# Every other load of expert weights is issued from ACT instead of SyncE

## The chip, the core and the metric

The kernel runs on one core of a Trainium2 chip. The core has a matrix engine (PE; its weight loads are shown apart as PEld), a vector engine (DVE), a scalar engine (ACT), GpSimd (POOL) and SyncE (SP), each with an instruction stream of its own that runs in order; they wait for one another through semaphores. DMAs bring data from HBM into the on-chip memory; the instruction that starts one stands in the stream of some engine, and in this kernel nearly all of them stand in SP's. The metric is the time of one execution in microseconds (us), as the median of several runs.

## The reference

Two residual layers over 256 tokens of width 1024. Each layer mixes tokens (a forgetting attention of 16 heads beside a gated recurrence of 8 heads), and then mixes channels. Layer 0 has a dense SwiGLU; layer 1, where the change lies, has eight SwiGLU experts of width 3584, of which each token uses its best two:

```
logits = (t @ w_router).astype(F32) + b_router.astype(F32)
top_val, top_idx = lax.top_k(logits, TOP_K)
top_w = jax.nn.softmax(top_val, axis=-1)
combine = jnp.sum(jax.nn.one_hot(top_idx, N_EXPERTS, dtype=F32) * top_w[..., None], axis=1)
for e in range(N_EXPERTS):
    out = out + combine[:, e:e + 1] * swiglu(t, w_gate[e], w_up[e], w_down[e]).astype(F32)
```

All weights are float32: one expert has three matrices of 1024 x 3584, some 44 MB, and all eight are read in full.

## The kernel before

Matrix products are made from float32 numbers split into a high and a low part, each in the format that PE multiplies at full rate. A piece of weights of 128 x 2048 numbers (1 MB) is loaded into a buffer `raw`; ACT casts a half of it (128 x 1024) to the high part `whi` (line 93), DVE subtracts that from `raw` to get the low part `wlo` (line 97), and PE multiplies with both (`mm3`, lines 113 to 115: high by high, high by low, low by high).

The experts are taken in an order set at run time, by how many tokens each has. Of the eight turns, those numbered 1, 4 and 7 (`FEW`) hold at most 64 tokens: there the high and the low part of the tokens share one block of 128 columns, and a weight needs two products instead of three (lines 1502, 1503, 1525, 1526). They are called the short turns here, the other five the long turns.

The experts' work is one list, `parts`, of 332 pieces, each of 1 MB of weights: for a block of 1024 hidden columns four parts of the gate matrix ("g"), four of the up matrix ("u"), and four of the down matrix of the block before ("d"). The function `run` writes the instructions out in a fixed order. In pass m it emits the products of part m, then the cast and the subtraction for the first half of part m + 2, then those for its second half; small operations (activation, transposes, gather, scatter) are hooked in between at three slots. `whi` and `wlo` have four buffers each, that is, two parts.

The buffers `raw` form a ring of 13 in the experts' stage. The load of part m + 13 overwrites the buffer of part m, so it waits for DVE's subtraction of the second half of part m, the last reader. The function `loads` emits, at the end of each pass, whatever loads have become possible; all of them stand in SP's stream (line 86). When the list comes to a new expert, SP reads that expert's number from memory into a register (line 1795), from which the addresses follow.

Of the kernel before, what the change touches and what calls it, by code (L numbers as in the profile page):

```python
# [10 lines left out]
F32 = mybir.dt.float32  # L11
# [6 lines left out]
P = 128  # L18
D = 1024
# [8 lines left out]
NE = 8  # L28
# [12 lines left out]
def hybrid_trunk_kernel(  # L41
# [6 lines left out]
    nc = tc.nc  # L48
# [16 lines left out]
    ring = [[wraw], 0, []]  # L65

    def raw_tile():
        pools = ring[0]
        j = ring[1] % sum(n for _, _, n, *_ in pools)
        if ring[1] and not j and ring[2]:  # L70
            pool, tag, bufs = ring[2].pop(0)
            return pool.tile([P, 2048], F32, tag=tag, bufs=bufs, name="raw")
        ring[1] += 1
        for pool, tag, n, *bufs in pools:
            if j < n:
                return pool.tile([P, 2048], F32, tag=tag, bufs=(bufs or [n])[0], name="raw")
            j -= n

    def load_raw(src, nk, n, step=None):
        raw = raw_tile()  # L80
        if nk * n == 2048:
            raw = raw.rearrange("p (k n) -> p k n", k=nk)
        else:
            raw = raw.rearrange("p (k n) -> p k n", k=max(4, nk))[:, :nk, :n]
        for k in range(0, nk, step or nk):
            nc.sync.dma_start(out=raw[:, k:k + (step or nk)], in_=src[:, k:k + (step or nk)])
        return raw

    def halves(raw, room=None):

        hi, lo = room or (wp.tile([P, 2, 512], F32R, tag=t, bufs=NSP, name=t) for t in ("whi", "wlo"))
        hi, lo = hi[:, :raw.shape[1], :raw.shape[2]], lo[:, :raw.shape[1], :raw.shape[2]]
        a.copy(hi, raw)  # L93
        return raw, hi, lo

    def lower(raw, hi, lo):
        v.tensor_sub(lo, raw, hi.bitcast(F32))  # L97

    def pairs_of(w):
        return [(w[1][:, j], w[2][:, j]) for j in range(w[1].shape[1])]  # L100
# [1114 lines left out]
    def moe(l, gate0):  # L1215
        with tc.tile_pool(name="moe", bufs=1, reuse_waits="tile") as mp:
# [130 lines left out]
            def an_expert(cl, w, **kw):  # L1347
                return dict(pos=cl[0], sel=cl[1], comb=cl[2], w=w, **kw)
# [84 lines left out]
            consts = {}  # L1433
# [247 lines left out]
            def run(exs):  # L1681
                parts, hooks = [], {}
# [5 lines left out]
                def hooked(key, slot):  # L1688
                    for f, args in hooks.pop((key, slot), ()):
                        f(*args)  # L1690
# [24 lines left out]
                for at, (ex, J) in enumerate(order):  # L1715
                    e, nq = ex["e"], ex["blocks"][J][1] // 256
# [45 lines left out]
                e, w_ = ex["e"], ex["blocks"][last][1]  # L1762
# [8 lines left out]
                key = (e, last, "d", 1, 0)  # L1771
# [9 lines left out]
                raws, ws = {}, {}  # L1781
                nring, once = sum(n for _, _, n, *_ in ring[0]), len(ring[2])
                known = [exs[0]]

                def loads(done):

                    while len(raws) < len(parts):
                        m = len(raws)
                        n = m + 3
                        prev = n - nring - (once if n < 2 * nring + once else 0)  # L1790
                        if n >= nring + once and prev - 3 > done:
                            break
                        e = parts[m]["key"][0]
                        if e == len(known):
                            r = nc.values_load(consts["idi"][0:1, e:e + 1], engines=(mybir.EngineType.SP,), min_val=0, max_val=NE - 1)
                            exs[e]["w"] = [w[0, bass.ds(r, 1)].rearrange("o d f -> (o d) f") for w in (moe_w_gate, moe_w_up, moe_w_down)]
                            known.append(exs[e])
                        src = parts[m]["src"]()
                        if src.shape[1] == 2:
                            raws[m] = load_raw(src, 2, D).rearrange("p k (h n) -> p (k h) n", h=2)  # L1800
                        else:
                            raws[m] = load_raw(src, 4, 512, 2 if m >= len(parts) - LASTS else 4)

                def half(m, k):
                    if m < len(parts):
                        w = halves(raws[m][:, k:k + 2])
                        lower(*w)
                        ws.setdefault(m, []).extend(pairs_of(w))

                loads(-1)  # L1810
                for m in range(2):
                    half(m, 0)
                    half(m, 2)
                    loads(m)
                    if m == 0:
                        silu(exs[0], 0, 0)
                        times_up(exs[0], 0, 0)
                for m, p in enumerate(parts):
                    p["products"](ws.pop(m))
                    hooked(p["key"], 0)  # L1820
                    half(m + 2, 0)
                    hooked(p["key"], 1)
                    half(m + 2, 2)
                    hooked(p["key"], 2)
                    loads(m + 2)
# [4 lines left out]
            exs = [an_expert([[t[:, i, 0:1] for i in range(NT)] for t in (pos, sel, comb)], [w[0, 0] for w in (moe_w_gate, moe_w_up, moe_w_down)],  # L1830
                             e=0, few=False, blocks=narrow)]
            for e in range(1, NE):
                exs.append(an_expert([[consts[k][:, i, e:e + 1] for i in range(NT)] for k in ("pos", "sel", "comb")], None, e=e, few=e in FEW, blocks=wide))
            with tc.manual_schedule():
                begin(exs[:1])
                run(exs)
# [72 lines left out]
LASTS = 2  # L1909
# [26 lines left out]
```

## Time and profile before

| | |
|---|---|
| median of 3 runs | 1940.73 us (1937.63 to 1941.56) |
| the profiled execution | 1939.08 us |
| its span, first to last instruction | 1937.4 us |
| PE busy | 1806.3 us, 93% |
| DVE busy | 1588.0 us, 82% |
| ACT busy | 1310.3 us, 68% |
| HBM read | 522.72 MB |

Busy time is time in which an engine runs instructions; issuing a DMA and waiting are not counted. A busy share over the whole span mixes stages with different limits, so the rows further down are taken from stretches of the experts' stage, which runs from about 936 to 1926 us. The program has the same instructions on PE, DVE and POOL before and after.

### The profile page before, as it was taken

To read this page: it belongs to the slowest core of one execution; us is meant where nothing else is said; L and a number is where in the kernel's file an instruction comes from. 1 tells how busy PE (TensorE), PEld (TensorE's weight loads), DVE (VectorE), ACT (ScalarE), POOL (GpSimd) and SP (SyncE) were. 2 spreads that over 40 slices of the span, in tenths; PEclk is the share of its full clock that TensorE was granted. 3 is DMA by queue.
4 is the path that set the end of the run, shared out by engine and by line. 5 is a ranking of instruction groups with operands and counts; after the bars stand their busy time and mean duration, and the time that the engine had idled before them with its cause. 6 is when DMAs were issued, how large, how long until landed. Compare 5 with 4: busy or idle time off the path is not lost. (4 is left out here: it accounts for less than half of the span.)

```text
span 1937.4 us, 25438 instructions
## 1 busy us (share of the span) xinstructions
PE 1806.3 (93%) x9038; PEld 1445.8 (75%) x9038; DVE 1588.0 (82%) x2061; ACT 1310.3 (68%) x1688; POOL 226.8 (12%) x214
## 2 busy tenths in 40 slices
PE   2999999999999999999999889999998899999887
PEld 2787787889978877788786557888865578878554
DVE  6877865878857877457888999989999999898997
ACT  2466568554445665685678778777787877777785
POOL 6701100000000012000211000310003200011000
PEclk9999999999999999999899999999999999999999
DMA  9534554788945425336989999989999899999991
GB/s 298 185 134 152 196 174 151 284 303 302 320 183 186 144 89 172 109 136 256 348 298 337 348 357 389 355 325 360 371 364 341 318 374 368 364 361 332 353 361 53
DMA packets 171399, 525.50 MB, mean 271 GB/s; under 512 B 11756, under 2 KB 23292, under 8 KB 157184
## 3 DMA queue, kind: packets, MB, share of 16 engines
q1 hardware_dynamic: 169880, 523.61, 75.1%
q8 instruction: 73, 1.20, 0.2%
q14 instruction: 62, 0.51, 0.1%
q10 hardware_dynamic: 1384, 0.18, 0.1%
HBM read 522.72 MB, written 1.05 MB: 270 GB/s over the span
## 5 line engine op out<-in xcount | busy, mean ns | idle before, releaser
L97 DVE TENSOR_TENSOR wlo<-raw,whi 128x1024 fp32r<-128x1024 f32 (+1 forms) x888 | 1071.2, 1237 | 142.2 <-ACT whi L93 132.5
L93 ACT CAST whi<-raw 128x1024 fp32r<-128x1024 f32 (+1 forms) x888 | 907.4, 1046 | 302.9 <-PE acc L115 160.4
L114 PE MATMUL acc<-wlo,g 128*128 128x512 f32 x544 | 213.8, 393 | 4.9 <-DVE wlo L97 4.9
L113 PE MATMUL acc<-whi,hTh 128*128 128x512 f32 x512 | 211.5, 415 | 4.4 <-ACT hTh L615 4.1
L113 PE MATMUL acc<-whi,g 128*128 128x512 f32 x544 | 215.2, 396 | 0.0
L114 PE MATMUL acc<-wlo,hTh 128*128 128x512 f32 x512 | 208.0, 407 | 6.3 <-DVE wlo L97 6.2
L115 PE MATMUL acc<-whi,g 128*128 128x512 f32 x544 | 213.1, 392 | 0.0
L115 PE MATMUL acc<-whi,hTl 128*128 128x512 f32 x512 | 208.8, 408 | 3.4 <-DVE hTl L617 3.4
L1503 PE MATMUL acc<-wlo,g 128*128 128x512 f32 x336 | 144.3, 430 | 32.8 <-DVE wlo L97 32.5
L1502 PE MATMUL acc<-whi,g 128*128 128x512 f32 x336 | 134.7, 401 | 1.2 <-ACT whi L93 1.2
L1503 PEld LDWEIGHTS acc<-wlo,g 128*128 128x128 f32 x336 | 63.0, 188 | 87.2 <-DVE wlo L97 77.9
L114 PEld LDWEIGHTS acc<-wlo,g 128*128 128x128 f32 x544 | 102.7, 189 | 29.3 <-DVE wlo L97 8.9
L115 PEld LDWEIGHTS acc<-whi,g 128*128 128x128 f32 x544 | 102.5, 188 | 21.5
L114 PEld LDWEIGHTS acc<-wlo,hTh 128*128 128x128 f32 x512 | 98.6, 193 | 26.8 <-DVE wlo L97 9.1
L113 PEld LDWEIGHTS acc<-whi,g 128*128 128x128 f32 x544 | 102.6, 189 | 20.8
L411 PE MATMUL acc<-hTh,whi 128*128 128x256 f32 x416 | 117.4, 282 | 0.0
L413 PE MATMUL acc<-hTh,wlo 128*128 128x256 f32 x416 | 116.7, 281 | 0.0
L412 PE MATMUL acc<-hTl,whi 128*128 128x256 f32 x416 | 116.6, 280 | 0.0
L115 PEld LDWEIGHTS acc<-whi,hTl 128*128 128x128 f32 x512 | 97.9, 191 | 24.7 <-DVE hTl L617 5.3
L113 PEld LDWEIGHTS acc<-whi,hTh 128*128 128x128 f32 x512 | 97.7, 191 | 23.7 <-ACT hTh L615 5.0
L114 PE MATMUL yb<-wlo,th 128*128 128x512 f32 x280 | 111.8, 399 | 2.2 <-DVE wlo L97 2.2
L302 POOL TENSOR_TENSOR rs<-rs,mhalf 128x8 f32<-128x8 f32 (+1 forms) x28 | 50.9, 1818 | 532.0 <-DVE rs L301 502.4
(421 smaller groups left out, 3203.6 us busy)
## 6 DMA issues: line engine op xcount, KB each, us to landing
raw<-in_moe_w_gate SPq DMA_DIRECT2D x112, 1024.0 KB, 7.3
raw<-in_moe_w_up SPq DMA_DIRECT2D x112, 1024.0 KB, 7.0
raw<-in_moe_w_down SPq DMA_DIRECT2D x110, 1024.0 KB, 6.9
raw<-in_w_in SPq DMA_DIRECT2D x66, 1024.0 KB, 5.1
raw<-in_w_ada SPq DMA_DIRECT2D x48, 1024.0 KB, 6.6
raw<-in_dense_w_gate SPq DMA_DIRECT2D x10, 1024.0 KB, 8.4
raw<-in_dense_w_up SPq DMA_DIRECT2D x10, 1024.0 KB, 7.5
raw<-in_dense_w_down SPq DMA_DIRECT2D x10, 1024.0 KB, 8.5
```

The lines of the kernel that those rows point to most:

```text
L93: a.copy(hi, raw)
L97: v.tensor_sub(lo, raw, hi.bitcast(F32))
L113: pe.matmul(out=o, lhsT=lh, rhs=rh, start=start, stop=False)
L114: pe.matmul(out=o, lhsT=lh, rhs=rl, start=False, stop=False)
L115: pe.matmul(out=o, lhsT=ll, rhs=rh, start=False, stop=stop)
L302: g.tensor_tensor(out=r, in0=r, in1=mhalf[:, :shape[1]], op=OP.pow)
L411: pe.matmul(out=o, lhsT=hi, rhs=hT.hh[:, k], start=(k == 0 and c % 2 == 0), stop=False)
L412: pe.matmul(out=o, lhsT=hi, rhs=hT.hl[:, k], start=False, stop=False)
L413: pe.matmul(out=o, lhsT=lo, rhs=hT.hh[:, k], start=False, stop=(k == KD - 1 and c % 2 == 1))
L1502: pe.matmul(out=o, lhsT=ex["g"][:, k], rhs=hi, start=(k == 0), stop=False)
L1503: pe.matmul(out=o, lhsT=ex["g"][:, k], rhs=lo, start=False, stop=(k == KD - 1))
```

## The change

`loads` is split into two queues. Each odd part from 13 on is loaded by an instruction in ACT's stream, every other part by one in SP's as before. The ring, the buffers and the sizes stay; the buffer of a part is now computed from its number, because the two queues no longer take them strictly in turn.

```
+                    raws[m] = raw.rearrange("p (k n) -> p k n", n=512)
+
+                turns_of = [m + 3 >= nring + once and m % 2 for m in range(len(parts))]
+
+                def loads(done, second=0):
+
+                    while at[second] < len(parts):
+                        m = at[second]
+                        if turns_of[m] == second:
+                            if needs(m) > done:
+                                break
+                            load(m, (nc.sync, nc.scalar)[second])
+                        at[second] += 1
...
                     p["products"](ws.pop(m))
                     hooked(p["key"], 0)
                     half(m + 2, 0)
+                    loads(m + 1, 1)
                     hooked(p["key"], 1)
                     half(m + 2, 2)
                     hooked(p["key"], 2)
                     loads(m + 2)
```

`needs(m)` is the number of the part that had the buffer last, so in the steady state m - 13. The new call stands between the two halves of a pass: in pass m, with m odd, ACT gets its cast for the first half of part m + 2, then the load of part m + 14, then the cast for the second half. That load waits for DVE's subtraction of the second half of part m + 1. ACT also reads each new expert's number into a register of its own (line 1797).

On ACT, in the first block of the short turn 4, the stream had six casts in a row between the activation of line 1556 and the copy of line 1564:

```order
L1556 ACTIVATE hid<-hid 64x1024
L93 CAST whi<-raw 128x1024 x6
L1564 COPY ug<-acc 64x512
L93 CAST whi<-raw 128x1024
L1564 COPY ug<-acc 64x512
```

and now has at the same place, with ISA the register arithmetic for the address:

```order
L1556 ACTIVATE hid<-hid 64x1024
L93 CAST whi<-raw 128x1024 x2
L1810 ISA
L1810 DMA raw<-in_moe_w_down 128x2048
L93 CAST whi<-raw 128x1024 x4
L1810 ISA
L1810 DMA raw<-in_moe_w_down 128x2048
L1564 COPY ug<-acc 64x512
L93 CAST whi<-raw 128x1024
L1564 COPY ug<-acc 64x512
```

Two loads have come in, four casts apart; the casts themselves have kept their order.

On SP, where the loads pass from one expert to the next (the fourth time), the stream had

```order
L86 DMA raw<-in_moe_w_down 128x2048
L1795 TENSOR_LOAD rank
L1795 ISA x2
L86 ISA
L86 DMA raw<-in_moe_w_gate 128x2x1024
L86 ISA
L86 DMA raw<-in_moe_w_gate 128x2x1024
L86 ISA
L86 DMA raw<-in_moe_w_gate 128x2x1024
```

and now has

```order
L1810 DMA raw<-in_moe_w_down 128x2048
L1797 TENSOR_LOAD rank
L1797 ISA x2
L1810 ISA
L1810 DMA raw<-in_moe_w_gate 128x2x1024
L1810 ISA
L1810 DMA raw<-in_moe_w_gate 128x2x1024
L1810 ISA
L1810 DMA raw<-in_moe_w_up 128x2x1024
```

The gate matrix now comes as two loads on SP, with two more on ACT, where it came as four on SP. In all 161 load instructions stand on ACT: 160 odd parts from 13 to 331, the last of them in two halves.

## Rows read from the trace of the kernel before

**Rows 1.** The page: busy time of each engine.
```profile
PE 1806.3 (93%) x9038; PEld 1445.8 (75%) x9038; DVE 1588.0 (82%) x2061; ACT 1310.3 (68%) x1688; POOL 226.8 (12%) x214
```
**Rows 2.** Stretches, long, short, whole stage: length, busy PE, PEld, DVE, ACT, POOL, clock, DMA.
```profile
1330.00:1420.00 90.00, 89.70 (x402) 73.70 (x401) 83.67 (x80) 70.45 (x76) 3.11 (x2) 1.00 0.98 359
1455.00:1547.00 92.00, 74.60 (x287) 50.38 (x285) 84.32 (x83) 72.66 (x92) 26.31 (x14) 0.94 0.92 331
936.50:1926.00 989.50, 920.34 (x3923) 700.95 (x3921) 906.99 (x888) 775.45 (x885) 101.20 (x63) 0.99 0.92 339
```
**Rows 3.** Waits of PE, 936 to 1926: total us, times, longest us.
```profile
PE acc L1503 <- DVE wlo L97: 32.5, 52, 1.2
PE yb L1526 <- DVE wlo L97: 21.1, 19, 1.9
...
PE acc L114 <- DVE wlo L97: 4.9, 7, 2.2
```
**Rows 4.** Waits of ACT, the two longest, and of DVE, 936 to 1926.
```profile
ACT whi L93 <- PE acc L115: 53.3, 139, 2.9
ACT whi L93 <- PE yb L115: 48.8, 109, 1.7
...
DVE wlo L97 <- ACT whi L93: 71.7, 121, 2.8
```
**Rows 5.** Waits of SP, the longest, 936 to 1926.
```profile
SPq L86 <- DVE wlo L97: 755.3, 314, 9.3
```
**Rows 6.** Line 86, 936 to 1926: ns min/median/max of an issue; last, us to landing.
```profile
L86 SPq DMA_DIRECT2D raw<-in_moe_w_down x112: 328/345/384, 949.5 to 1887.5; - x112
...
L86 SPq DMA_DIRECT2D raw<-in_moe_w_gate x103: 368/383/412, 936.2 to 1864.3; - x103
...
DMA to landing us min/median/max: 4.8/7.0/8.9
```
**Rows 7.** Timeline of ACT around 26: start us, us, engine, line, work.
```profile
26.26 0.43 ACTq L235 DMA_DIRECT2D og<-in_hg_o_gain  x1
26.38 1.04 ACT L93 CAST whi<-third 128x1024 fp32r<-128x1024 f32 x1
...
27.19 0.46 ACTq L237 DMA_DIRECT2D wr<-in_w_router  x1
27.69 1.04 ACT L93 CAST whi<-raw 128x1024 fp32r<-128x1024 f32 x1 [0.27 <-issue]
```
**Rows 8.** Timeline of DVE, SP and ACT around 1441, short turn 4.
```profile
1440.25 1.23 DVE L97 TENSOR_TENSOR wlo<-raw,whi 128x1024 fp32r<-128x1024 f32 x1 [0.93 <-ACT whi L93]
...
1441.50 0.35 SPq L86 DMA_DIRECT2D raw<-in_moe_w_down  x1
...
1441.07 1.04 ACT L93 CAST whi<-raw 128x1024 fp32r<-128x1024 f32 x1
...
1442.53 1.22 DVE L97 TENSOR_TENSOR wlo<-raw,whi 128x1024 fp32r<-128x1024 f32 x1
```
**Rows 9.** Timeline of DVE and ACT around 1047, the first late place.
```profile
1046.49 1.22 DVE L97 TENSOR_TENSOR wlo<-raw,whi 128x1024 fp32r<-128x1024 f32 x1
...
1048.02 0.59 ACT L1594 CAST th<-tb 128x512 fp32r<-128x512 f32 x1
...
1049.58 1.23 DVE L97 TENSOR_TENSOR wlo<-raw,whi 128x1024 fp32r<-128x1024 f32 x1 [0.41 <-ACT whi L93]
```
**Rows 10.** Timeline of DVE and ACT around 1874, the last late place.
```profile
1873.77 1.22 DVE L97 TENSOR_TENSOR wlo<-raw,whi 128x1024 fp32r<-128x1024 f32 x1
...
1872.82 0.58 ACT L1551 COPY hid<-acc 64x512 f32<-64x512 f32 x1
...
1873.30 1.04 ACT L93 CAST whi<-raw 128x1024 fp32r<-128x1024 f32 x1
...
1876.63 1.21 DVE L97 TENSOR_TENSOR wlo<-raw,whi 128x1024 fp32r<-128x1024 f32 x1
```
**Rows 11.** Line 1795: ns min/median/max, first and last start.
```profile
L1795 SPq TENSOR_LOAD <-rank x7: 263/278/486, 1005.8 to 1756.0; - x7
```

More of the change, by code (lines that the diff above doesn't have):

```diff
@@ L1783, in run @@
                 known = [exs[0]]
[L1785 to L1802, printed above, removed]
+                slots = [(pool, tag, (bufs or [n])[0]) for pool, tag, n, *bufs in ring[0] for _ in range(n)]
@@ new lines, in run, with needs, load @@
+                at = [0, 0]
+                def needs(m):
+                    n = m + 3
+                    return n - nring - (once if n < 2 * nring + once else 0) - 3 if n >= nring + once else -1
+                def load(m, queue):
+                    e = parts[m]["key"][0]
+                    while e >= len(known):
+                        k = len(known)
+                        r = nc.values_load(consts["idi"][0:1, k:k + 1], engines=(mybir.EngineType.SP, mybir.EngineType.Activation), min_val=0, max_val=NE - 1)
+                        exs[k]["w"] = [w[0, bass.ds(r, 1)].rearrange("o d f -> (o d) f") for w in (moe_w_gate, moe_w_up, moe_w_down)]
+                        known.append(exs[k])
+                    src = parts[m]["src"]()
+                    nk, n = src.shape[1:]
+                    if m + 3 < nring + once:
+                        raw = raw_tile()
+                    else:
+                        pool, tag, bufs = slots[(m + 3 - once) % nring]
+                        raw = pool.tile([P, 2048], F32, tag=tag, bufs=bufs, name="raw")
+                    o = raw.rearrange("p (k n) -> p k n", n=n)
+                    step = nk // 2 if m >= len(parts) - LASTS else nk
+                    for k in range(0, nk, step):
+                        queue.dma_start(out=o[:, k:k + step], in_=src[:, k:k + step])
+                    raws[m] = raw.rearrange("p (k n) -> p k n", n=512)
```

## The prediction

> **What bounds the kernel now.** I read the page first [rows 1]: PE is busy for 1806 of 1937 us, but that share mixes stages. The change touches only the experts' stage, so the next view is the busy time in stretches of it [rows 2]. In a long turn PE has 89.70 of 90 us and DVE 83.67: PE is the bound, DVE is 93% full. In a short turn PE has only 74.60 of 92 and DVE 84.32: two products per weight are not enough to fill PE, and the subtractions set the pace. The waits say the same [rows 3]: PE waits for `wlo` for 53.6 us (32.5 + 21.1) at the lines of the short turns, and for 4.9 us at line 114, which the long turns use. ACT, at 78 or 79% of both, waits for PE to give `whi` buffers back [rows 4].
>
> Are the loads late? ACT's longest waits name PE and no load [rows 4]. The 332 parts take 989.5 us [rows 2], 2.98 us each. A load is issued when part m - 13 has been subtracted, some 12 parts or 36 us before its cast, and lands after 7.0 us, at most 8.9 [rows 6]: some 27 us to spare. SP stands waiting for free buffers for 755 us of the stage [rows 5]. What the loads wait for is DVE, not a queue.
>
> **What the change removes.** 161 issues of 0.35 to 0.38 us [rows 6], some 60 us, leave SP. They lay beside SP's 755 us of waiting, so they are worth nothing. The same loads on a second queue are worth nothing either while 27 us are spare; a load that ACT issues up to a microsecond or two late has the same cover. Seven reads of an expert's number come to ACT, 0.28 us each on SP [rows 11]; each stands between two casts of 1.05 us, under which the stream can run ahead, so I cost them at 0 (without that cover, 7 times the longest, 0.49: 3.4 us). SP's read of the overflow count moves forward among its loads, behind a value that is by then written: 0.
>
> **What it adds: a wait in ACT's stream.** ACT works in order. Call the cast before the load k. The load waits for the subtraction of half k - 1, and the cast k + 1 and everything after stand behind it. Before, ACT could run ahead of DVE: in [rows 8] the cast k + 1 starts at 1441.07, while DVE is still at subtraction k - 1. At every fourth half it now may not.
>
> How long does an issue hold ACT? Between subtraction and load 0.02 to 0.03: the subtraction of [rows 8] ends at 1441.48, and SP's load, which waited for just that, starts at 1441.50. The issue itself 0.38 (the same loads on SP, rows 6). To the next instruction 0.04: in [rows 7] an issue on ACT ends at 27.65, the cast behind it starts at 27.69. Sum 0.45 us after the subtraction's end. Those rows show also that an issue that needn't wait costs ACT nothing (one of 0.43 at 26.26 runs into the cast from 26.38), and bound the issue on ACT: 0.43 to 0.46 for small tensors.
>
> One place worked out, short turn 4 [rows 8]. Subtraction k - 1 ends at 1441.48; the cast k + 1, at 1441.07 before, can now start at 1441.93, ends after 1.04 at 1442.97, and its subtraction starts at 1443.00 instead of 1442.53: DVE is 0.47 late. In general DVE has the subtraction k (1.14 from start to start) to do while ACT needs 0.45 + 1.05 + 0.03, so some 0.4 are lost, unless DVE has another operation in between, on hidden columns or outputs; and more where ACT has other work between the load and the cast.
>
> So I laid each of the 160 places against the trace like this: subtraction's end + 0.45, then ACT's operations at their old spacing, against the old start of the subtraction they feed.
> - Short turns, 57 places: 29 come late, at 1046 us for the first and 1874 for the last. The first [rows 9]: subtraction ends 1047.71, the cast of line 1594 goes from 1048.02 to 1048.16, 0.14 late, and DVE was waiting there anyway, so all of it counts. The last [rows 10]: ends 1874.99, the copy of line 1551 from 1872.82 to 1875.44, the cast 0.48 behind it ends at 1876.96, DVE starts at 1876.99 instead of 1876.63: 0.36. Of the 29, 21 lose up to 0.5 (9.1 us together), eight lose 0.6 to 1.7 (7.0 us). The other 28 are covered by DVE's own extra work. As PE waits for DVE here, the 16.1 us go to the end.
> - Long turns, 103 places: 53 subtractions come late, by 21 us in all, but PE hardly waits for them there [rows 3], and DVE has 6.3 us idle in each 90 [rows 2] to win it back. By the same laying-out PE waits at three places: 2.2 us.
>
> Sum 18.3 us, on the profiled execution's own 1939.08 (span 1937.4 and 1.7 around it): 1957.4. That execution lies 1.65 us below the median of the three runs, 1940.73, within their spread. I take 1958.
>
> **Bounds.** From below: with the shortest issue of [rows 6], 0.33, the price is 0.40, and the same laying-out gives 14.7 + 2.0, or 1956; if DVE's other idle time takes in two thirds of that, 1945; if all of it, nothing is lost. From above: an issue of 0.46 as in [rows 7] gives 18.6 + 2.7, and ACT's lateness carried past the following load some 5 more, 1965. If an issue took twice 0.38, 30.5 + 5.3 and up to 20 more in the long turns, whose slack would then be eaten: 1975 to 1995.
>
> **Rivals.**
> - *No change* (1937 to 1944). It would need ACT's lead to be large enough that the subtraction is done when the load comes up. In the long turns it nearly is; in the short turns the casts run ahead of DVE by more than one half [rows 8], which speaks against it: the load asks for what DVE has not done yet. The Trainium skill says (DMA: Bandwidth & Descriptors, "Issuing engines are not separate DMA queues") that DMAs from several engines share the same 16 DMA engines and that issuing from several saves only the sequencer's issue time; by that rule alone the sum would be 0. The trace agrees on what can be gained (SP's issue time is idle time), and adds the price that the rule leaves out.
> - *Faster* (about 1930): two queues keep more data in flight, loads land sooner, and DVE's and ACT's idle time shrinks. It decides if casts wait for landings. For it: the DMA share is 0.92 to 0.98 in all stretches [rows 2]. Against it: 27 us to spare, and waits that name PE. A fifth of PE's 53.6 us would be worth 10.
> - *Much slower* (1970 to 1995): the two streams issue at once and hold each other up, or DVE in the long turns, 93% full, falls so far behind that PE waits there too. 103 places x 0.47 is 48 us at most; DVE has some 43 us idle there (7% of 206 parts at 2.98 us, 614 us), so it takes more than the single price. The skill states (Perfetto Trace Analysis, "DMA Instruction — HWDGE (DVE, Sync)") that the sequencer itself sits out the semaphore wait and then a lock on a descriptor generator that two sequencers share. By that a collision would add one more issue; SP's loads wait for a subtraction two halves after ACT's, so I expect few, and no run here shows one.
>
> **How the numbers follow.** The forecast (1945 to 1970) gets 0.62, much slower 0.20, no change 0.12, faster 0.06. Faster or slower by under 0.2% (3.9 us) is what a measurement can't tell from nothing. From the cases: faster 0.06, within 0.2% 0.10 (no change, with a little of it and of the forecast's low end on either side), slower 0.84. The range that leaves out 2 in 10 is 1942 to 1982.
>
> **What would show it.** In the profile after: ACT idle behind loads of line 1810, with the issue at about 0.38 and the next cast some 0.45 after a subtraction's end; DVE's waits for `whi`, 71.7 us before [rows 4], up by 30 or more, PE's waits for `wlo` up by about 16 at lines 1503 and 1526 and by little at line 114; short turns longer by some 5 to 6 us each, long ones by under 1; loads still landing in about 7 us. The prediction is wrong if the short turns keep their length, if the long turns lengthen as much as the short ones, or if ACT's issues take another time than SP's.

## The result and the profile after

The changed kernel takes 1957.53 us (median of 4 runs, 1956.16 to 1961.15), the kernel before 1939.75 beside it (4 runs, 1937.63 to 1941.56): a ratio of 1.0104, 95% interval 1.009 to 1.0118. It is slower, by 17.8 us between the medians and 20.2 by the ratio. The forecast was 1958. The profiled execution took 1958.6 us, its span is 1956.8.

First the page of the profile after: the same instructions as in [rows 1], and nearly the same busy times. So no engine works longer; something waits. The two lines of queues (packets, MB, share of the 16 DMA engines' span) show that the loads are split: before, the first queue had 75% and the second next to nothing. First after, then before:

```profile
PE 1809.1 (92%) x9038; PEld 1442.7 (74%) x9038; DVE 1588.4 (81%) x2061; ACT 1302.6 (67%) x1688; POOL 219.8 (11%) x214
...
q1 hardware_dynamic: 129416, 355.83, 51.3%
q10 hardware_dynamic: 41848, 167.97, 23.4%
```
```profile
q1 hardware_dynamic: 169880, 523.61, 75.1%
...
q10 hardware_dynamic: 1384, 0.18, 0.1%
```

Next the waits of the experts' stage after, to hold against [rows 3] and [rows 4] (us in total, times, longest). One line was next to nothing before: ACT waits for DVE's `wlo` before a cast, 53.0 us in 48 places, where it was 1.0 in 3 (the last line shown here, of before). DVE in turn waits 29.6 us longer for `whi` (101.3 against 71.7), and PE longer for `wlo` at the lines of the short turns, while line 114 hardly moves. ACT's two waits for PE have shrunk from 102 to 63 us: it has lost its lead.

```profile
DVE wlo L97 <- ACT whi L93: 101.3, 161, 2.6
...
ACT whi L93 <- DVE wlo L97: 53.0, 48, 2.3
...
PE acc L1503 <- DVE wlo L97: 41.6, 67, 1.2
ACT whi L93 <- PE yb L115: 32.5, 52, 2.4
ACT whi L93 <- PE acc L115: 30.7, 75, 4.3
PE yb L1526 <- DVE wlo L97: 22.6, 23, 1.9
...
PE acc L114 <- DVE wlo L97: 5.7, 9, 2.2
```
```profile
ACT whi L93 <- DVE wlo L97: 1.0, 3, 0.3
```

The loads themselves, at line 1810 from 936 us on (issue in ns, min/median/max; the last line is us from issue to landing). An issue takes ACT as long as SP within some 0.01 us, and loads land no later than in [rows 6] by the median (6.4 against 7.0 us; the latest after 10.0 against 8.9); SP waits for free buffers even longer than in [rows 5].

```profile
L1810 ACTq DMA_DIRECT2D raw<-in_moe_w_down x56: 347/352/391, 947.9 to 1905.4; - x56
L1810 ACTq DMA_DIRECT2D raw<-in_moe_w_up x53: 374/379/422, 938.2 to 1886.8; - x53
L1810 ACTq DMA_DIRECT2D raw<-in_moe_w_gate x52: 379/390/410, 937.7 to 1880.7; - x52
L1810 SPq DMA_DIRECT2D raw<-in_moe_w_up x52: 367/373/384, 939.4 to 1884.0; - x52
...
DMA to landing us min/median/max: 4.7/6.4/10.0
```
```profile
SPq L1810 <- DVE wlo L97: 848.6, 154, 12.2
```

Last the timeline of ACT and DVE after (start, us, engine, line, work, idle before), at the place of [rows 8]. Before, ACT's casts ran ahead of DVE there. Now ACT has two casts and then stands until the subtraction that began at 1445.55 ends, at about 1446.78; the load starts at 1446.81, the next cast at 1447.20, and DVE, done with two subtractions, is idle for 0.37 us before the third. The sum worked out for this place was 0.47 late. Five us later the second load costs next to nothing: the copy behind it waits for PE anyway, which lets it go as the issue ends.

```profile
1444.49 1.98 ACT L93 CAST whi<-raw 128x1024 fp32r<-128x1024 f32 x2
1446.81 0.35 ACTq L1810 DMA_DIRECT2D raw<-in_moe_w_down  x1
1447.20 3.90 ACT L93 CAST whi<-raw 128x1024 fp32r<-128x1024 f32 x4 [0.74 <-DVE wlo L97]
1451.81 0.35 ACTq L1810 DMA_DIRECT2D raw<-in_moe_w_down  x1
1452.26 0.58 ACT L1564 COPY ug<-acc 64x512 f32<-64x512 f32 x1 [1.16 <-PE yb L115]
```
```profile
1445.55 2.36 DVE L97 TENSOR_TENSOR wlo<-raw,whi 128x1024 fp32r<-128x1024 f32 x2 [0.93 <-ACT whi L93]
1448.28 4.63 DVE L97 TENSOR_TENSOR wlo<-raw,whi 128x1024 fp32r<-128x1024 f32 x4 [0.37 <-ACT whi L93]
```

Over 160 such places, worked out from the starts and ends in the trace: the load starts 0.03 us after the subtraction k - 1, takes 0.38, and ACT's next instruction starts 0.46 us after that subtraction (medians).

Where the time went by turn, each from the end of its first part's subtractions to the same point of the next turn (us; turn 7 up to the end of the last subtraction, which is the last column):

| | start | 0 | **1** | 2 | 3 | **4** | 5 | 6 | **7** | end |
|---|---|---|---|---|---|---|---|---|---|---|
| before | 940.2 | 107.5 | 128.6 | 125.6 | 121.7 | 129.1 | 120.1 | 125.9 | 127.3 | 1926.0 |
| after | 936.0 | 109.5 | 134.5 | 126.7 | 121.4 | 136.6 | 121.1 | 125.8 | 133.7 | 1945.3 |

The short turns (bold) are 5.9, 7.5 and 6.4 us longer, 19.8 together; the five long ones 3.7 together. The stage is 23.5 us longer, but it began 4.2 us earlier: that part of the program is the same in both kernels, and its start varies between 935 and 943 us over the profiled executions of all the runs below, so it is not put down to the change.

### The profile page after: what moved, and what is told of

Same layout as the page of the kernel before. It is cut to its first block, busy times and chain, and to the rows that moved or that the text cites. A ratio compares the mean times of both kernels' runs of the same rounds, so it can differ in the third digit from the quotient of the medians.

```text
span 1956.8 us, 25375 instructions
## 1 busy us (share of the span) xinstructions
PE 1809.1 (92%) x9038; PEld 1442.7 (74%) x9038; DVE 1588.4 (81%) x2061; ACT 1302.6 (67%) x1688; POOL 219.8 (11%) x214
## 3 DMA queue, kind: packets, MB, share of 16 engines
HBM read 522.72 MB, written 1.05 MB: 268 GB/s over the span
## 4 chain that ended last, share of the span: by engine, by line
PE 51%; DVE 13%; issue 7%; ACT 7%; POOL 1%; ACTq 1%; DVEq 0%; POOLq 0%
DVE wlo L97 9%; PE acc L115 8%; PE acc L114 8%; PE acc L113 8%; ACT whi L93 4%; PE yb L114 3%; PE yb L115 3%; PE yb L113 2%; PE acc L412 2%; PE acc L411 2%; PE acc L413 2%; PE yb L1526 2%; PE acc L1503 1%; PE tb L308 1%; PE yb L1525 1%
## 5 line engine op out<-in xcount | busy, mean ns | idle before, releaser
L115 PE MATMUL yb<-whi,tlo 128*128 128x512 f32 x280 | 111.1, 397 | 0.0
```

Source lines behind the costliest of these rows:

```text
L115: pe.matmul(out=o, lhsT=ll, rhs=rh, start=False, stop=stop)
```

## The experiments

The theory: **what costs is ACT's wait for a subtraction that is not yet done, 0.46 us from its end to ACT's next work, and only where DVE is needed at once.** Rivals: the issues themselves take ACT's time; two queues disturb the loads; each load on ACT costs the same everywhere. Medians and ratios are against the kernel before on the same chip (1936.63, then 1936.66, then 1935.72 us).

**The load behind the second cast of its pass.** It asks for the same subtraction, which is then k - 2.

```
                     half(m + 2, 0)
-                    loads(m + 1, 1)
                     hooked(p["key"], 1)
                     half(m + 2, 2)
                     hooked(p["key"], 2)
+                    loads(m + 1, 1)
                     loads(m + 2)
```

> The load on ACT waits for the same subtraction as in the change, but stands one cast later in ACT's stream: behind the second half's cast of the pass. The cast behind the load can then start 0.45 us after the subtraction of k - 1 and ends 1.5 us after it, while DVE has two subtractions (2.28 us) to do meanwhile. Theory: no late subtraction, 1937 to 1946 us. Rival 1 (issue time on ACT) and rival 2 (two queues): 1950 to 1960 as in the change.

Measured: 1937.8 us (11 runs), ratio 0.9997, 0.9988 to 1.0007. The same 161 issues on ACT, of the same length, the same two queues, the same register reads, and no cost. In its waits DVE's is back where it was in [rows 4], and PE's two at their old size; ACT still waits for `wlo` at some places, where it does no harm. Half of the loads, 81 of 160, still start within 0.05 us of the end of the subtraction that they wait for: ACT does stand there, but DVE has another subtraction to do meanwhile.

```profile
DVE wlo L97 <- ACT whi L93: 71.4, 119, 2.8
...
PE acc L1503 <- DVE wlo L97: 29.4, 45, 1.2
PE yb L1526 <- DVE wlo L97: 23.1, 20, 1.9
...
ACT whi L93 <- DVE wlo L97: 16.7, 14, 2.9
```

That rules out the issue time and the second queue, for harm and for gain, in one run. One cast's distance decides.

**ACT's call one pass later.**

```
-                    loads(m + 1, 1)
+                    loads(m, 1)
```

> The same loads on ACT, but each one part later in the list: in pass m ACT issues the load whose buffer was freed by part m instead of part m + 1, so the load waits for the subtraction of half k - 3 instead of k - 1, where k is the cast ahead of it. The number of issues on ACT (161) and the two queues are unchanged. Theory (ACT's in-order wait for DVE is the cost): the subtraction is done when the load comes up, the issue runs under the cast before it; 1936 to 1944 us, as before the change, and ACT waits for no subtraction. Rival 1 (the issues themselves cost ACT, 161 x 0.45 = 72 us of its stream, of which 24 us reach the end): still 1950 to 1960. Rival 2 (two queues disturb the transfers or the engines' memory access): still 1955 to 1960.

Measured: 1947.26 us (5 runs), ratio 1.005, 1.0036 to 1.0064. By the expectation this spoke against the theory. But the kernel did not do what was meant. Eight of the 13 buffers share a name ("tag") with others, and those of one tag are handed out in the order of the calls. With ACT's call alone moved, SP's load of the next part came first and took the buffer meant for ACT's, so that ACT got the later one. That can happen to 63 of the 160 loads; in the trace 59 of these 63 start 0.03 us after the subtraction k - 1, as in the changed kernel, while of the other 97 only 25 find their own subtraction not done. 63/160 of 20 us is 8: most of what was measured.

**Both calls one pass later**, so that each buffer goes to its own part, with ACT's load still between the two casts, but asking for k - 3:

```
-                    loads(m + 1, 1)
+                    loads(m, 1)
...
-                    loads(m + 2)
+                    loads(m + 1)
```

> As the changed kernel, with both calls one pass later: ACT's load of part m + 13 is still between the two casts of a pass, but it is now emitted in pass m, not m - 1, so the subtraction it waits for lies two halves further back (k - 3 in place of k - 1); SP's loads are emitted one pass later too, so that each buffer goes to its own part. In the run with ACT's call alone moved, 59 of 63 loads whose buffer shares a tag with the next part's had got the next part's buffer and still started 0.03 us after the subtraction k - 1. Theory (ACT pays only where it asks for a subtraction that isn't done): 0 to 4 us over the kernel before, waits of ACT's casts for wlo, 53.0 us in the changed kernel, under 15. Rival (the place between two casts is what costs): 8 us or more over it, whatever subtraction is waited for. Rival (parts arrive late when loaded one pass later): ACT or DVE waiting for DMAs of raw.

Measured: 1938.42 us (12 runs), ratio 1.0004, 0.9993 to 1.0015; DVE's wait for `whi` is back, ACT's for `wlo` is gone, and the one wait for a load is 0.3 us. The place between the casts is innocent, and loading one pass later makes nothing late. Even here 38 of the 160 loads start within 0.05 us of the subtraction that they ask for, and it costs nothing.

```profile
DVE wlo L97 <- ACT whi L93: 73.3, 121, 2.8
...
ACT whi L93 <- DVE wlo L97: 0.7, 2, 0.3
...
ACT whi L93 <- DMA raw<-in_moe_w_down: 0.3, 1, 0.3
```

**Every part on ACT, or every fourth.**

```
-  turns_of = [m + 3 >= nring + once and m % 2 for m in range(len(parts))]
+  turns_of = [m + 3 >= nring + once for m in range(len(parts))]
```

> Every part from 13 on is loaded from ACT at the place that the change uses (320 loads instead of 161 issues, one in each pass). Theory: the places' losses laid out on the trace before the change double to 26 us in the short turns and 6 in the long ones; scaled by the 24 us that the experts' stage really took instead of 18, 32 to 43 us: 1970 to 1984 us. Rival 2 (two queues): a single queue again for nearly all loads, 1936 to 1945.

Measured: 2001.13 us (4 runs), ratio 1.033, 1.0314 to 1.0346: 64 us by the ratio, above the range. Twice the places cost three times as much, at the same price of a place (0.45 us). But some 9 of the 64 us are of another kind: early in the first turn ACT stands for 4.6 and 4.3 us until an earlier load has landed, as told below for all parts asking for k - 3. Without the first turn the stage is 50.8 us longer, against 21.6 in the changed kernel: 2.4 times. The waits:

```profile
DVE wlo L97 <- ACT whi L93: 142.4, 230, 4.5
ACT whi L93 <- DVE wlo L97: 82.8, 96, 3.8
PE acc L1503 <- DVE wlo L97: 45.7, 76, 1.2
...
ACT th L1594 <- DMA raw<-in_moe_w_gate: 4.6, 1, 4.6
...
ACT whi L93 <- DMA raw<-in_moe_w_up: 4.3, 1, 4.3
```

With `m % 4 == 1`, 80 loads on ACT:

> Every fourth part (13, 17, 21, ...) from ACT, 80 loads, at the place that the change uses. Theory: the losses of these places laid out on the trace before are 7.4 + 0.4 us, scaled as above 8 to 11: 1946 to 1952 us. Rival 2 (two queues at all): 1950 to 1958.

Measured: 1947.3 us (5 runs), ratio 1.0049, 1.0035 to 1.0063, as expected: 9.5 us, half of the change's 20, so between 80 and 160 places the cost goes with their number.

**ACT loads in the long turns only.**

```
-  turns_of = [m + 3 >= nring + once and m % 2 for ...
+  turns_of = [m + 3 >= nring + once and m % 2 and parts[m - 12]["key"][0] not in FEW for ...
```

> As the changed kernel, but ACT loads only where the place stands in a long turn, about 103 loads; in the short turns SP loads everything. Theory (ACT's delay reaches the end only where PE waits for DVE): 1 to 6 us over the kernel before, with the short turns as long as before; the changed kernel's long turns together are 3.7 us longer. Rival (each load on ACT costs the same wherever it stands): 103/161 of 20 us, 12 or more.

Measured: 1941.99 us (10 runs), ratio 1.002, 1.0006 to 1.0034: 4 us, for 103 of the 161 loads. The three short turns take 128.1, 129.4 and 127.4 us, as before. Each load on ACT does not cost the same: the 57 places in the short turns carry most of it.

**Two issues behind the wait.** ACT's loads come in two halves of 0.5 MB.

```
-  step = nk // 2 if m >= len(parts) - LASTS else nk
+  step = nk // 2 if m >= len(parts) - LASTS or turns_of[m] else nk
```

> As the changed kernel, with each of ACT's loads in two halves of 0.5 MB, so that two issues of some 0.35 to 0.38 us follow the wait instead of one. Theory (the price of a place is the issue after the awaited subtraction): the price goes from 0.46 to some 0.85 us, by the laying-out of the prediction twice the loss in the short turns and a little more than twice in the long ones, 33 to 45 us over the kernel before: 1970 to 1985. Rival (the handover between DVE and ACT costs, the issue runs beside it): within 4 us of the changed kernel, 1954 to 1962.

Measured: 2030.25 us (4 runs), ratio 1.0475, 1.0455 to 1.0495. That is 92 us, twice what was expected or more. The price of a place was nearly as foreseen: 0.34 for each issue, 0.18 between them, 0.94 in all (median of 160). The timeline of one place in short turn 4:

```profile
1487.24 2.36 DVE L97 TENSOR_TENSOR wlo<-raw,whi 128x1024 fp32r<-128x1024 f32 x2 [0.93 <-ACT whi L93]
...
1488.50 0.98 ACTq L1810 DMA_DIRECT2D raw<-in_moe_w_down  x2
...
1489.52 3.90 ACT L93 CAST whi<-raw 128x1024 fp32r<-128x1024 f32 x4 [1.37 <-PE acc L1503]
...
1490.60 4.63 DVE L97 TENSOR_TENSOR wlo<-raw,whi 128x1024 fp32r<-128x1024 f32 x4 [1.00 <-ACT whi L93]
```

The load starts when the first of the two subtractions ends, at 1488.47; ACT's next cast starts 1.05 later, and DVE is idle for 1.00 before what it feeds. (The cast's row names PE as its releaser; but the two issues end at 1489.48, right before the cast starts, so they held it until then in any case.) The long turns, which the change left nearly alone, are now 8 to 11 us longer each. Long turn 6 of this kernel, and of the one before (length, busy PE, PEld, DVE, ACT, POOL, clock, DMA share, GB/s):

```profile
1745.50:1879.70 134.20, 129.32 (x576) 101.49 (x575) 111.58 (x105) 93.95 (x113) 10.06 (x8) 1.00 0.93 328
```
```profile
1672.80:1798.70 125.90, 125.00 (x576) 103.08 (x575) 112.25 (x104) 98.09 (x114) 14.72 (x8) 1.00 0.96 351
```

PE has 4.9 us in which it does nothing, against 0.9, and is busy for 4.3 us more with the same 576 products at the same clock. Two readings were left: a longer price falls due in full once the cover is gone, or 320 issues fill ACT itself. So two more runs, of the kernel with both calls one pass later.

**Two issues, asking for k - 3:**

> The kernel with both calls one pass later (ACT's load asks for the subtraction k - 3), now with each of ACT's loads in two halves, so that it issues 320 of them. The same two issues behind the subtraction k - 1 made 93 us. What was not expected there is either that a longer price falls due in full once DVE's idle time is used up, or that the issues fill ACT itself: 160 x some 0.9 us = 144 us more in a stage of 990 in which ACT is busy for 776. Theory (only issues that begin after an awaited subtraction count): 0 to 12 us over the kernel before. Rival (ACT is too full with them): 40 us or more.

Measured: 1938.26 us (10 runs), ratio 1.001, 0.9994 to 1.0025. The same 320 issues: 92 us behind k - 1, nothing that can be measured behind k - 3. DVE's wait for `whi` is 74.3 us in 130 places, and each turn is within 1.1 us of its old length.

**All parts on ACT, asking for k - 3:**

> The kernel with both calls one pass later, with all parts from 13 on loaded by ACT, one issue in each pass. The same at the subtraction k - 1 made 64 us. Theory: 0 to 12 us over the kernel before, as nearly no load asks for a subtraction that is not done. Rival (ACT is too full with 320 issues of 0.38 us): 40 us or more.

Measured: 1946.36 us (6 runs), ratio 1.0055, 1.0034 to 1.0075. Within the 12 us, but not by a cost at each load: the first turn takes 118.3 us instead of 107.5, and all later ones are within 0.2 of before, though 68 of its loads still start within 0.05 us of the subtraction that they ask for. The timeline of ACT shows the two places, at the start of the stage, where a load holds ACT for 5 us and more. What these two wait for is no subtraction but, as the profile says, a landing: the load at 949.39 signals its own landing on the same semaphore as the load at 937.61, and ACT first waits for that one to land, at 949.03, 11.4 us after its issue. The load at 956.48 waits in the same way for the one at 938.13, which lands at 956.40. ACT had issued four loads in a row here, from 936.65 on, and the last two of them landed late:

```profile
936.65 0.93 ACTq L1810 DMA_DIRECT2D raw<-in_moe_w_gate  x2
937.61 1.43 ACTq L1810 DMA_DIRECT2D raw<-in_moe_w_up  x2
...
949.39 0.37 ACTq L1810 DMA_DIRECT2D raw<-in_moe_w_up  x1
949.80 1.99 ACT L93 CAST whi<-raw 128x1024 fp32r<-128x1024 f32 x2 [5.70 <-DMA raw<-in_moe_w_up]
956.48 0.35 ACTq L1810 DMA_DIRECT2D raw<-in_moe_w_down  x1
956.88 0.60 ACT L1549 ACTIVATE hid<-acc 128x512 f32<-128x512 f32 x1 [5.08 <-DMA raw<-in_moe_w_up]
```

**The second queue on GpSimd**, which has the time (`nc.gpsimd` for `nc.scalar`, and the register read with it):

> As the changed kernel with the second queue on GpSimd instead of ACT, the same 160 odd parts at the same places. Theory (the cost is ACT's wait, not the second queue): 0 to 6 us over the kernel before; ACT's casts wait for wlo as little as before; GpSimd's few operations of an expert (one-hot, outputs) now stand behind loads, up to one pass of 3 us later, mostly with time to spare. Rival (two queues in flight disturb the loads or the engines): 15 us or more over the kernel before, as with ACT.

Measured: 1944.79 us (8 runs), ratio 1.0042, 1.0029 to 1.0055: 8 us, a little over the range. ACT and DVE are free of it, as the theory has it: DVE's wait for `whi` is 72.1 us. What grew lies elsewhere. The subtractions of the stage take 1246 ns in the mean instead of 1237, 6 us over 664 of them. Subtractions that run long (over 1.28 us) are all beside GpSimd's own operations, as before, but the 14 beside its addition at line 1613 lose 12.5 us now and lost 7.1. That addition comes at other moments, since it stands behind loads, and it is slower too; of before, then of this kernel (mean ns of one behind the busy time):

```profile
L1613 POOL TENSOR_TENSOR ys<-yg,ys 128x512 fp32r<-128x512 f32 x14 | 21.5, 1539 | 556.9 <-ACT ys L1609 357.7 <-PE acc L115 113.3 <-issue 85.9
```
```profile
L1613 POOL TENSOR_TENSOR ys<-yg,ys 128x512 fp32r<-128x512 f32 x14 | 24.1, 1722 | 0.3
```

That this is the cause of the 8 us was not tried. No version was faster than the kernel before.

## Why the prediction was right, point by point

- *The loads aren't late, so SP's relief and the second queue are worth nothing.* Shown: with both in place and the load one cast later, the time is that of before. The rival "faster" falls with it. The rule of the Trainium skill that the prediction weighed (DMA: Bandwidth & Descriptors, "Issuing engines are not separate DMA queues"), that issuing from several engines saves only the sequencer's issue time, agrees with that run as to the gain, which is none here.
- *The price of a place, 0.03 + 0.38 + 0.04 = 0.45 us.* Measured 0.46 in the changed kernel. ACT's issue of 1 MB took 0.35 to 0.39, as SP's.
- *The wait is what costs.* Shown three ways: k - 2 and k - 3 cost nothing, and 320 issues behind k - 3 cost nothing that can be measured. "No change" would have been right for a kernel in which ACT asked one cast later.
- *Seven register reads on ACT cost nothing.* They are there in the k - 2 version too, 0.28 us each by the median.
- *Short turns 16.1, long turns 2.2.* Measured 19.8 and 3.7. Both terms were too small, by a fifth and by two fifths: 23.5 instead of 18.3. Of the long turns the first is 2.0 longer and two others 1.1 and 1.0, where under 1 was expected; short turn 4 is 7.5 longer, where 5 to 6 were. The profiled execution came out where it was forecast (1958.6 against 1957.4) because the stage began 4.2 us earlier; the medians differ by 17.8, the ratio stands for 20.2. So the sign, the mechanism and the division among turns were right, and the agreement to a microsecond was luck.
- *PE's waits at lines 1503 and 1526 up by about 16, DVE's for `whi` by 30 or more.* DVE's rose by 29.6. PE's rose by 10.6 only, though the short turns grew by 19.8. In these turns PE is also busy for 8 us more (334.2 against 326.2, with the same products), at a granted clock of 0.97, 0.91 and 0.97 against 0.99, 0.96 and 0.97. Together that is 18.6. But PE's busy time also grew in long turn 6 of the run with two issues, where the clock stayed at 1.00, so the clock needn't be the reason. For turn 1 a run tells whether longer products add to the time. With the load behind the second cast PE is busy there for 111.40 us, as long as in the changed kernel (111.46; before 109.15), and the turn takes 129.7 us (before 128.6) and not 134.5. So by this run at most 1.1 of the 5.9 us lost in turn 1 come with the longer products, which for the most part fill what would else be waiting. For turns 4 and 7 this stays open. Turn 1 of the changed kernel, then with the load behind the second cast (columns as above):

```profile
1045.50:1180.00 134.50, 111.46 (x414) 71.94 (x413) 122.80 (x121) 100.20 (x114) 3.10 (x2) 0.97 0.95 343
```
```profile
1045.50:1175.20 129.70, 111.40 (x416) 75.77 (x415) 121.67 (x121) 102.29 (x117) 3.10 (x2) 0.95 0.97 354
```
- *"Much slower", by two streams that issue at once.* Not seen in the changed kernel: of the 161 issues on ACT none overlaps one of SP's. But with two issues asking for k - 3, 48 of ACT's 320 do, 15 of them for 0.33 us or more. In these 15 SP's issue takes 0.37 to 0.39 us, as long as when it is alone, and ACT's 0.45 by the median, two of them 0.97 and 1.19; ACT's issues that overlap none take 0.34. So a collision cost ACT some 0.1 us, rarely more, and the run as a whole nothing that can be measured. One of them, ACT and SP:

```profile
1242.70 1.02 ACTq L1810 DMA_DIRECT2D raw<-in_moe_w_gate  x2
```
```profile
1243.24 0.39 SPq L1810 DMA_DIRECT2D raw<-in_moe_w_up  x1
```

By the lock that the prediction cited from the Trainium skill (Perfetto Trace Analysis, "DMA Instruction — HWDGE (DVE, Sync)") a collision would add one more issue, some 0.37 us; 13 of these 15 don't show that, as ACT's took at most 0.22 longer. In the run with two issues 31 of ACT's 320 took over 0.5 us, up to 1.15, each the second of its pair and none beside an issue of SP's; why is open.
- *The step that failed is the size at another price.* The prediction gave 30.5 + 5.3, and up to 20 more in the long turns, for an issue of twice 0.38; measured were 92, at a price of 0.94. By turns, in the changed kernel, with every part on ACT and with two issues: the three short ones are longer by 19.8, 30.7 and 46.7 us, the four long ones behind the first by 1.8, 20.1 and 37.2, the first by 2.0, 12.5 and 7.7. So the short turns became 1.6 and 2.4 times as costly, for twice the places and twice the price, and the larger part of the surprise lies in the long turns, whose slack was used up; the prediction named that, but its term for them, at most 25.3, was too small, and its 30.5 for the short ones too. Its laying-out set each place against the old trace, as if DVE had won back the last place's delay by then. A sum over all places comes nearer to what was measured. By the prediction's own terms a place makes a subtraction late by the price less 0.06 (1.14 for DVE's work against 1.05 + 0.03 beside the price). That is an estimate:

| kernel | places x late | sum | measured | taken in |
|---|---|---|---|---|
| every other part | 160 x 0.40 | 64 | 20 | 44 |
| every part | 320 x 0.39 | 125 | 64 | 61 |
| two issues | 160 x 0.88 | 141 | 92 | 49 |
| long turns only | 103 x 0.40 | 41 | 4 | 37 |
| every fourth part | 80 x 0.40 | 32 | 9.5 | 22 |

DVE had 82.5 us idle in the stage before [rows 2]. In the three rows with the most delay 44 to 61 of that were used, or 70 for every part without its 9 us of waits for landings. From 0.46 to 0.94 a place, the 160 places cost 72 us more, 0.45 each, of 0.48 added: nearly one for one. From 160 to 320 places 61 us of delay were added and 44 us of time, 35 without the waits for landings. So the table fits both misses on size in kind, but it gives no fixed stock of slack; it was made after those runs and was not tested by a further one, so this part is argued and not shown.

## What to carry to other kernels

A DMA in the stream of an engine that computes is free here as long as the engine that frees its buffer has other work ready meanwhile, even if the DMA has to wait (at k - 2 half of the loads did, at no cost); it costs its handover and its issue where that engine needs the next piece at once. So choose the place by the age of the release it asks for (here k - 1 costs 20 us, k - 2 and k - 3 nothing), not by how busy the engine is. Before moving loads to a second queue, see if anyone waits for a landing; here SP stood idle and nobody did. Slack covers such delays only until it is used up, so a cost measured at one size doesn't scale: in four long turns 1.8 us became 20.1 with twice the places and 37.2 with twice the price, and the whole became more than four times as much at twice the price.

## What the runs showed that was not expected

- An issue on GpSimd takes longer than on ACT or SP: 0.56 us for down and 0.72 for gate and up by the median, against 0.35 and 0.38 to 0.39 on ACT.
- Half the bytes are not half an issue: 0.34 us for 0.5 MB, 0.35 to 0.39 for 1 MB, and 0.18 us pass between two such issues in a row.
- In which order loads are called can decide which buffer each gets, and so what it waits for: moving one of two calls changed the release for 59 of 160 loads.
